# The low halves of a weight stream: an adding DMA from GpSimd's queue instead of a subtraction on VectorE

## The chip, the cores and the metric

One core of one Trainium2 chip runs the whole kernel. The metric is the device time of one execution in microseconds, lower is better; it was run three times before the change. The engines are named as the profile names them: PE is TensorE (its weight loads are PEld), DVE is VectorE, ACT is ScalarE, POOL is GpSimd, SP is SyncE, whose queue issues the DMAs of the kernel before.

## What is computed

Two layers of a diffusion transformer over 256 context tokens and 256 latent tokens with 1024 features. A layer is a feed-forward half step, a hybrid mixer (a gated linear recurrence, latent attention and neighbourhood attention) and a second feed-forward half step. In the last layer the context is not needed behind the mixer, so the second feed-forward there runs on the 256 latents alone. Cut to what matters here:

```python
for layer in range(2):
    last = layer == 1
    h  = h  + 0.5 * g1  * swiglu(modulate(rms_norm(h),  sh1,  sc1),  ffn1_w_in, ffn1_w_out)
    hc = hc + 0.5 * cg1 * swiglu(modulate(rms_norm(hc), csh1, csc1), ffn1_w_in, ffn1_w_out)
    yc, yl = hybrid_mixer(..., need_ctx=not last)
    h  = h  + gm * yl
    h  = h  + 0.5 * g2 * swiglu(modulate(rms_norm(h), sh2, sc2), ffn2_w_in, ffn2_w_out)
    if not last:
        hc = hc + cgm * yc
        hc = hc + 0.5 * cg2 * swiglu(modulate(rms_norm(hc), csh2, csc2), ffn2_w_in, ffn2_w_out)
return h
```

The weights are float32. Every product runs on TensorE in the type float32r, which keeps fewer bits. So each weight block is split into a high part, the weight rounded to float32r, and a low part, the weight less its high part, and each activation likewise. A product is three matmuls: high by high, high by low and low by high.

## The kernel before

All weights lie in memory as one stream of 128x128 blocks, in the order of use. `chunks` cuts it into 316 chunks of up to 8 blocks, a [128, 1024] float32 tile of 512 KB each; the chunks are numbered 0 to 315. The last feed-forward holds chunks 250 to 315, the output projection of the second layer's mixer chunks 241 to 249, the input projections of that mixer 223 to 241.

A chunk goes through `Stream` in three steps. `load` (line 327) issues one DMA on SP's queue into one of three `wraw` tiles. `split_hi` (line 334) casts it on ScalarE into a `whi` tile. `split_lo` (line 340) subtracts the high part from the raw tile on VectorE into a `wlo` tile (GpSimd may take it for the first six chunks). `whi` and `wlo` come from a ring of five pairs. The raw tile is free for the next load behind the subtraction; a ring pair is free when TensorE has read the chunk's last block. `mm3` (lines 628 to 630) makes the three matmuls of a block: `wh` by `h`, `wh` by `lo`, `wl` by `h`.

A block's three matmuls move 512 columns where both kinds of tokens are worked on, and 256 or 258 in the layer-1 output projection and in the last feed-forward, which have the latents alone. Each block there is taken from the ring once.

Beside the stream, the modulation vectors are made by `gemv`: a [128, 1024] tile `graw` of `w_mod` comes by a DMA on SP's queue, and VectorE multiplies it with silu(c) twice with a sum (`junk`, line 680). There are 144 such tiles, spread over the first three feed-forwards and the start. GpSimd takes the few powers of the norms (`rr`, `rq`, line 743) and some sums of squares (`acc`, line 723).

The order of each engine's instructions is fixed when the program is built. `Weave` runs a small model of the engines over programs of steps, each with an engine, a cost, the events it waits for and fires and the slots it takes and gives (`raw` 3, `ring` 5), and emits the step that could start first or is most urgent. On the chip each engine then works through its queue in that order, with semaphores for the waits.

Of the kernel before, what the change touches and what calls it, by code (L numbers as in the profile page):

```python
# [24 lines left out]
AF = mybir.ActivationFunctionType  # L25
# [21 lines left out]
# ---------------------------------------------------------------- layout of the weight stream  # L47

def out_tiles(l, w):
    """Tiles of a feed-forward output, by what is worked on together: the latents alone leave little time per tile."""  # L50
    return ((0, 1),) + tuple((dt,) for dt in range(2, KT)) if (l, w) == (L - 1, 2) else tuple((dt,) for dt in range(KT))


def plan():
    """The order of 128-wide weight blocks in the stream: (key, blocks side by side)."""
# [36 lines left out]
def uses(key):  # L92
    """How often the blocks of a key are taken from the ring."""
# [17 lines left out]
def chunks(pl):  # L111
    """Cut the stream into chunks of up to CH blocks; no group straddles two chunks."""
# [159 lines left out]
def pack_gates(a):  # L272
    """Two 64-wide blocks on the diagonal of each 128 x 128 tile: [layer, tile, 128, dir, a or x, 128]."""
# [28 lines left out]
# ---------------------------------------------------------------- the kernel  # L302

class Stream:
    """Weights in order of use: DMA, then the exact split into two float32r parts."""
# [30 lines left out]

    def split_lo(self, i, eng):
# [14 lines left out]
class Step:  # L352
    """One step of a program: its engine and cost (or several that could do it), what it emits, the events it waits
    for and fires (when its data lands, lag later), the slots it takes first and gives back."""
# [7 lines left out]
class Weave:  # L362
    """Interleaves programs (generators of steps) in the order in which a model of the engines runs them.

    A step may run once its events have fired and its slots are free; of those that could start first on an
    engine, the one of the most urgent program is emitted. Each engine then issues in the order of emission.
    """

    LATENCY = {"PE": 0.2, "ACT": 0.135, "DVE": 0.135, "POOL": 0.19, "DMA": 0.0}
# [22 lines left out]
    def pace(self, t):  # L392
        """The tensor engine's clock halves after a window of little work, until a window of full work."""
# [6 lines left out]
    def start(self, p):  # L400
        """(start, program, engine, cost) of the next step, or None."""
# [85 lines left out]
def emit(tc, xT, cc, wmod, wst, cols_d, cst_d, nab, gates, wm0, ccol, out, layers=L):  # L487
# [3 lines left out]
    with es:  # L491
# [30 lines left out]
        def S(*a, **k):  # L522
            return Step(*a, **k)
# [1252 lines left out]
```

## Time and profile before

| | |
|---|---|
| three runs | 1764.41, 1761.28, 1764.37 us, median 1764.37 |
| span of the profiled execution, first to last instruction | 1759.8 us (its time as a run is not listed apart; the median stands 4.6 us above the span) |
| PE busy | 1735.3 us, 99% |
| DVE busy | 1194.3 us, 68% |
| ACT busy | 696.3 us, 40% |
| POOL busy | 82.8 us, 5% |
| DMA, mean share of 16 engines | 41% on queue q1, 143 GB/s |

The busy shares are means over stages that differ. Two kinds of answers are read below: the busy times of every engine within a stretch of the span, and the DMA queue of such a stretch, whose share is that of 16 DMA engines and whose rate in GB/s stands beside it. A matmul's busy time overlaps with that of its neighbours, so PE's pace is read from the number of matmuls in a stretch.

### The profile page before, as it was taken

To read this page: it belongs to the slowest core of one execution; us is meant where nothing else is said; L and a number is where in the kernel's file an instruction comes from. 1 tells how busy PE (TensorE), PEld (TensorE's weight loads), DVE (VectorE), ACT (ScalarE), POOL (GpSimd) and SP (SyncE) were. 2 spreads that over 40 slices of the span, in tenths; PEclk is the share of its full clock that TensorE was granted. 3 is DMA by queue.
4 is the path that set the end of the run, shared out by engine and by line. 5 is a ranking of instruction groups with operands and counts; after the bars stand their busy time and mean duration, and the time that the engine had idled before them with its cause. 6 is when DMAs were issued, how large, how long until landed. Compare 5 with 4: busy or idle time off the path is not lost.

```text
span 1759.8 us, 24027 instructions
## 1 busy us (share of the span) xinstructions
PE 1735.3 (99%) x9428; PEld 1426.8 (81%) x9428; DVE 1194.3 (68%) x1958; ACT 696.3 (40%) x1096; POOL 82.8 (5%) x68
## 2 busy tenths in 40 slices
PE   7999999999999999999999999999999999999999
PEld 4788888889766698888888898888888977699999
DVE  7898677636667778776775478776333667876564
ACT  4432122224667553221222252222222367764442
POOL 1100000000110010000000000000000111100000
PEclk9999999999999999999999999999999999999999
DMA  8554445322221126554553345444222132246653
GB/s 323 194 202 180 166 180 188 136 95 91 78 69 42 49 85 216 184 186 167 187 183 129 112 160 183 182 174 151 96 96 96 63 112 90 65 129 192 183 183 123
DMA packets 73589, 251.71 MB, mean 143 GB/s; under 512 B 9090, under 2 KB 12418, under 8 KB 73220
## 3 DMA queue, kind: packets, MB, share of 16 engines
q1 hardware_dynamic: 73476, 250.18, 41.0%
q8 instruction: 74, 1.21, 0.3%
q14 instruction: 39, 0.32, 0.1%
HBM read 249.10 MB, written 1.05 MB: 142 GB/s over the span
## 4 chain that ended last, share of the span: by engine, by line
PE 94%; DVE 3%; ACT 1%; issue 1%; POOL 0%; DMA 0%; SPq 0%; DVEq 0%; POOLq 0%; ACTq 0%
PE mm L628 27%; PE mm L629 27%; PE mm L630 27%; PE sc L1256 3%; PE tr L1282 1%; PE o L1326 1%; PE mm L1388 1%; DVE junk L1678 1%; PE tr L949 1%; PE o L628 1%; PE o L629 1%; PE o L630 1%; PE sc L1008 1%; PE mm L1507 1%; PE sc L628 1%
## 5 line engine op out<-in xcount | busy, mean ns | idle before, releaser
L628 PE MATMUL mm<-xh,whi 128*128 128x512 f32 (+2 forms) x1722 | 627.8, 365 | 2.6 <-ACT xh L770 2.5
L629 PE MATMUL mm<-xl,whi 128*128 128x512 f32 (+2 forms) x1722 | 613.2, 356 | 2.9 <-DVE xl L1461 1.6
L630 PE MATMUL mm<-xh,wlo 128*128 128x512 f32 (+2 forms) x1722 | 612.8, 356 | 0.0
L334 ACT CAST whi<-wraw 128x1024 fp32r<-128x1024 f32 (+1 forms) x316 | 330.4, 1046 | 666.9 <-PE mm L629 458.2
L340 DVE TENSOR_TENSOR wlo<-wraw,whi 128x1024 fp32r<-128x1024 f32 (+1 forms) x311 | 379.8, 1222 | 260.3 <-ACT whi L334 256.7
L628 PEld LDWEIGHTS mm<-xh,whi 128*128 128x128 f32 x1722 | 325.8, 189 | 65.7 <-issue 12.5
L629 PEld LDWEIGHTS mm<-xl,whi 128*128 128x128 f32 x1722 | 326.0, 189 | 55.8 <-issue 4.1
L630 PEld LDWEIGHTS mm<-xh,wlo 128*128 128x128 f32 x1722 | 325.7, 189 | 50.7
L680 DVE SCALAR_TENSOR_TENSOR junk<-graw,silc 128x1024 f32<-128x1024 f32 x256 | 312.7, 1221 | 4.9 <-DMA graw<-in_wmod_dram 0.5
L628 PE MATMUL mm<-hh,whi 128*128 128x512 f32 (+1 forms) x748 | 264.6, 354 | 0.0
L629 PE MATMUL mm<-hl,whi 128*128 128x512 f32 (+1 forms) x748 | 263.1, 352 | 0.0
L630 PE MATMUL mm<-hh,wlo 128*128 128x512 f32 (+1 forms) x748 | 262.2, 351 | 0.0
L630 PEld LDWEIGHTS mm<-hh,wlo 128*128 128x128 f32 x748 | 140.6, 188 | 21.8
L628 PEld LDWEIGHTS mm<-hh,whi 128*128 128x128 f32 x748 | 140.3, 188 | 21.3
L629 PEld LDWEIGHTS mm<-hl,whi 128*128 128x128 f32 x748 | 140.8, 188 | 20.5
L804 DVE SCALAR_TENSOR_TENSOR x<-mm,mod,x 128x256 f32<-128x256 f32 x158 | 71.2, 479 | 89.1 <-PE mm L630 88.6
L846 ACT CAST hh<-h 128x512 fp32r<-128x512 f32 (+1 forms) x88 | 49.7, 567 | 156.2 <-DVE h L834 133.8
L834 DVE TENSOR_TENSOR h<-sg,mm 128x512 f32<-128x512 f32 x62 | 42.6, 686 | 69.9 <-PE mm L630 69.3
L857 DVE TENSOR_TENSOR hl<-h,hh 128x512 fp32r<-128x512 f32 (+1 forms) x88 | 54.5, 623 | 33.0 <-ACT hh L846 32.8
L723 POOL TENSOR_TENSOR acc<-acc,nsq 128x256 f32<-128x256 f32 x18 | 19.1, 1064 | 1090.1 <-ACT nsq L719 1090.0
L1256 PE MATMUL sc<-m_kp,m_qp 128*128 128x512 f32 (+3 forms) x120 | 55.8, 546 | 1.5 <-ACT m_p L1273 1.0
L743 POOL TENSOR_TENSOR rr<-rv,nhalf 128x2 f32<-128x2 f32 (+2 forms) x29 | 37.6, 1304 | 320.0 <-DVE rv L736 243.1
(234 smaller groups left out, 1484.7 us busy)
## 6 DMA issues: line engine op xcount, KB each, us to landing
wraw<-in_wst_dram SPq DMA_DIRECT2D x308, 512.0 KB, 3.4
graw<-in_wmod_dram SPq DMA_DIRECT2D x137, 512.0 KB, 5.3
graw<-in_wm_dram SPq DMA_DIRECT2D x7, 512.0 KB, 7.2
x<-in_xT_dram SPq DMA_DIRECT2D x8, 256.0 KB, 5.3
nab<-in_nab_dram SPq DMA_DIRECT2D x16, 128.0 KB, 2.1
silc<-in_cc_dram SPq DMA_DIRECT2D x2, 1024.0 KB, 5.5
m_gw<-in_gates_dram SPq DMA_DIRECT2D x6, 256.0 KB, 2.7
out_dram<-x SPq DMA_DIRECT2D x8, 128.0 KB, 1.9
```

The source lines that it names most:

```text
L334: self.nc.scalar.copy(hi[:, :n], self.raws[i][:, :n])
L340: eng.tensor_tensor(lo[:, :n], self.raws.pop(i)[:, :n], hi[:, :n].bitcast(F32), OP.subtract)
L628: PE.matmul(o, wh[:, :m], h, start=start, stop=False)
L629: PE.matmul(o, wh[:, :m], lo, start=False, stop=False)
L630: PE.matmul(o, wl[:, :m], h, start=False, stop=stop)
L680: V.scalar_tensor_tensor(ph["junk"], g["r"], 1.0, ph["sc"][:, s, :], OP.mult, OP.mult, accum_out=mod[l, c][:, s, j:j + 1])
L743: G.tensor_tensor(r, v, e, OP.pow)
L804: yield S("DVE", 0.4, lambda: V.scalar_tensor_tensor(x[:, dt, half(s)], o[:, half(s)], gate[:, s, dt:dt + 1], x[:, dt, half(s)], OP.mult, ...
L834: V.tensor_tensor(g["h"][:, cs], g["s"][:, cs], pu[:, cs], OP.mult)
L846: A.copy(hs[f][0][:, cs], g["h"][:, hc])
L857: yield S("DVE", dve(n), lambda: V.tensor_tensor(hs[f][1][:, cs], g["h"][:, hc], hs[f][0][:, cs].bitcast(F32), OP.subtract), give={"h": 1} ...
L1256: PE.matmul(g["s"][:, :keys], q[r0:r1, ts(t)], kk[r0:r1, :keys], start=True, stop=True)
```

## The change

From chunk 12 on, the low part is made in two steps. ScalarE writes the negated rounded weight into `wlo`, straight from the raw tile, behind its cast into `whi`; then a DMA issued on GpSimd's queue adds the raw weights, read from memory a second time, to what lies in `wlo`. The raw tile is given back behind the negation. Chunks 0 to 11 keep the subtraction. In the planner the new DMA is a step of an engine of its own, SW, with a cost of 1.5 and a landing 3.0 later.

```diff
 class Stream:
+    def negate(self, i):
+        n = self.size(i)
+        hi, lo = self.tiles[i]
+        self.nc.scalar.activation(lo[:, :n], self.raws.pop(i)[:, :n], AF.Copy, scale=-1.0)
+
+    def add_raw(self, i):
+        n = self.size(i)
+        hi, lo = self.tiles[i]
+        src = bass.AP(tensor=self.src.tensor, offset=self.src.offset + self.off[i], ap=[[n, 128], [1, n]])
+        self.nc.gpsimd.dma_start(lo[:, :n], src, accum_op=OP.add)
...
-    LATENCY = {"PE": 0.2, "ACT": 0.135, "DVE": 0.135, "POOL": 0.19, "DMA": 0.0}
+    LATENCY = {"PE": 0.2, "ACT": 0.135, "DVE": 0.135, "POOL": 0.19, "DMA": 0.0, "SW": 0.0}
...
-SLACK = {"PE": 0.12, "ACT": 0.12, "DVE": 0.12, "POOL": 0.0, "DMA": 0.0}
+SLACK = {"PE": 0.12, "ACT": 0.12, "DVE": 0.12, "POOL": 0.0, "DMA": 0.0, "SW": 0.0}
...
+N_VECTOR = 12
...
         def split_hi(cs):
             for c in cs:
                 yield S("ACT", act(W.size(c)), lambda: W.split_hi(c), take={"ring": 1},
                         wait=[("raw", c)] + ([("hi", c - 1)] if c else []), fire=("hi", c))
+                if c >= N_VECTOR:
+                    yield S("ACT", act(W.size(c)), lambda: W.negate(c), give={"raw": 1}, fire=("nhi", c))

         def split_lo(cs):
             for c in cs:
                 n = W.size(c)
+                if c >= N_VECTOR:
+                    yield S("SW", 1.5, lambda: W.add_raw(c), wait=[("nhi", c)], fire=("chunk", c), lag=3.0)
+                    continue
                 yield S(("DVE", "POOL") if c < N_POOL else ("DVE",), (dve(n), 2.3), lambda e=None: W.split_lo(
                     c, G if e == "POOL" else V), wait=[("hi", c)], give={"raw": 1}, fire=("chunk", c))
```

Comments were taken out of the file as well, and the new lines shift the line numbers behind them. In the changed kernel the cast stays on line 334, the negation is line 341, the adding DMA line 348, the subtraction line 353.

ScalarE's queue in the last feed-forward, before (the silu of the gate is `sg`, the high part of the product `hh`):

```order
L334 CAST whi<-wraw 128x1024
L846 CAST hh<-h 128x256
L334 CAST whi<-wraw 128x1024 x2
L853 ACTIVATE sg<-sg 128x256
L334 CAST whi<-wraw 128x1024
L846 CAST hh<-h 128x256
```

and with the change:

```order
L334 CAST whi<-wraw 128x1024
L341 ACTIVATE wlo<-wraw 128x1024
L334 CAST whi<-wraw 128x1024
L872 ACTIVATE sg<-sg 128x256
L341 ACTIVATE wlo<-wraw 128x1024
L865 CAST hh<-h 128x256
```

Each cast of a chunk is followed by a negation of the same size, with at most a `sg` or a `hh` between them.

GpSimd's queue from the end of the layer-1 mixer to the end of the program, before:

```order
L743 TENSOR_TENSOR rr<-rv,nhalf 128x8
L743 TENSOR_TENSOR rq<-rv,nhalf 128x2
L723 TENSOR_TENSOR acc_12846<-acc_12846,nsq 128x256 x2
L743 TENSOR_TENSOR rr<-rv,nhalf 128x2
L1771 UNCONDITIONAL_BRANCH
```

and with the change:

```order
L762 TENSOR_TENSOR rr<-rv,nhalf 128x8
L348 DMA wlo<-in_wst_dram 128x1024 x2
L762 TENSOR_TENSOR rq<-rv,nhalf 128x2
L348 DMA wlo<-in_wst_dram 128x1024 x7
L762 TENSOR_TENSOR rr<-rv,nhalf 128x2
L348 DMA wlo<-in_wst_dram 128x1024 x61
L348 DMA wlo<-in_wst_dram 128x768
L1790 UNCONDITIONAL_BRANCH
```

The adding DMAs, 304 in all, now stand in GpSimd's queue between the powers; behind the last norm's power there are 62 in a row.

## Rows read from the trace of the kernel before

**Rows 1.** The page, parts 1 and 2: busy time by engine; 40 slices.

```profile
PE 1735.3 (99%) x9428; PEld 1426.8 (81%) x9428; DVE 1194.3 (68%) x1958; ACT 696.3 (40%) x1096; POOL 82.8 (5%) x68
...
PE   7999999999999999999999999999999999999999
...
DMA  8554445322221126554553345444222132246653
GB/s 323 194 202 180 166 180 188 136 95 91 78 69 42 49 85 216 184 186 167 187 183 129 112 160 183 182 174 151 96 96 96 63 112 90 65 129 192 183 183 123
```

**Rows 2.** Stretches: us, busy us by engine (instructions), PE clock, DMA share, GB/s.

```profile
88.00:308.00 220.00, 220.00 (x942) 176.91 (x941) 172.97 (x260) 56.90 (x68) 0.00 (x0) 1.00 0.51 183
396.00:660.00 264.00, 263.46 (x1627) 203.34 (x1626) 184.96 (x374) 162.86 (x303) 29.36 (x25) 1.00 0.20 69
660.00:924.00 264.00, 264.00 (x1169) 214.12 (x1168) 200.24 (x294) 71.80 (x91) 0.00 (x0) 1.00 0.52 187
1056.00:1232.00 176.00, 176.00 (x754) 141.51 (x753) 129.73 (x191) 42.97 (x52) 0.00 (x0) 1.00 0.47 172
1232.00:1364.00 132.00, 132.00 (x565) 106.14 (x564) 46.02 (x54) 36.87 (x50) 1.46 (x1) 1.00 0.28 96
1364.00:1580.00 216.00, 209.91 (x1449) 170.75 (x1448) 158.77 (x316) 136.08 (x252) 26.94 (x23) 1.00 0.29 89
1540.00:1584.00 44.00, 43.50 (x349) 40.72 (x348) 34.77 (x69) 26.88 (x49) 2.47 (x3) 1.00 0.40 127
1584.00:1750.00 166.00, 166.00 (x1386) 166.00 (x1385) 104.51 (x150) 73.12 (x96) 0.00 (x0) 1.00 0.58 178
```

**Rows 3.** Waits of PE between 1364 and 1580 us: total, times, longest.

```profile
PE mm L629 <- DVE xl L1461: 1.6, 1, 1.6
PE sc L1256 <- ACT m_p L1273: 1.0, 1, 1.0
```

**Rows 4.** The page, part 5: groups of instructions, busy, mean ns, idle before.

```profile
L334 ACT CAST whi<-wraw 128x1024 fp32r<-128x1024 f32 (+1 forms) x316 | 330.4, 1046 | 666.9 <-PE mm L629 458.2
L340 DVE TENSOR_TENSOR wlo<-wraw,whi 128x1024 fp32r<-128x1024 f32 (+1 forms) x311 | 379.8, 1222 | 260.3 <-ACT whi L334 256.7
```

**Rows 5.** ACT in order of time, 1640 to 1648 us: start, duration, instruction.

```profile
1641.83 1.05 ACT L334 CAST whi<-wraw 128x1024 fp32r<-128x1024 f32 x1 [1.83 <-PE mm L629]
1644.71 1.05 ACT L334 CAST whi<-wraw 128x1024 fp32r<-128x1024 f32 x1 [1.83 <-PE mm L629]
```

**Rows 6.** Waits of ACT between 1584 and 1756 us: total, times, longest.

```profile
ACT whi L334 <- PE mm L629: 46.7, 27, 1.8
...
ACT whi L334 <- DMA wraw<-in_wst_dram: 2.4, 2, 1.3
```

**Rows 7.** DMA queues and issues between 12 and 27 us; last figure us to landing.

```profile
DMA packets 1721, 6.20 MB, mean 413 GB/s; under 512 B 190, under 2 KB 210, under 8 KB 1721
...
q1 hardware_dynamic: 1721, 6.20, 102.7%
...
wraw<-in_wst_dram SPq DMA_DIRECT2D x3, 512.0 KB, 7.7
```

**Rows 8.** The same between 1232 and 1364 us.

```profile
q1 hardware_dynamic: 3456, 12.58, 27.4%
...
wraw<-in_wst_dram SPq DMA_DIRECT2D x23, 512.0 KB, 3.2
```

**Rows 9.** The same between 1584 and 1750 us.

```profile
DMA packets 8710, 29.62 MB, mean 178 GB/s; under 512 B 960, under 2 KB 1657, under 8 KB 8697
...
q1 hardware_dynamic: 8697, 29.42, 57.8%
...
wraw<-in_wst_dram SPq DMA_DIRECT2D x53, 512.0 KB, 3.5
```

**Rows 10.** POOL's instructions by shape over the span: busy, mean ns, idle before.

```profile
L340 POOL TENSOR_TENSOR wlo<-wraw,whi 128x1024 fp32r<-128x1024 f32 x5 | 13.4, 2684 | 23.6 <-ACT whi L334 23.6
...
L743 POOL TENSOR_TENSOR rr<-rv,nhalf 128x4 f32<-128x4 f32 x5 | 6.7, 1341 | 73.8 <-DVE rv L736 73.8
```

## Prediction

> **What bounds the kernel now.** I read the page first [rows 1]: PE is busy 99% of the span and in every slice but the first, while DVE, from which the change takes work, stands at 68%. So the first question is not how much DVE time goes, but whether PE ever waits for DVE or for a chunk. The waits of PE answer it: they are short. In the second mixer, the one stretch with gaps, PE is idle for 216.0 - 209.9 = 6.1 us [rows 2], and only two of its waits reach 1 us [rows 3]. None of them is for a `wlo`. That is all that a relieved DVE can give back outside the start and the end.
>
> The second question is the pace at which PE eats chunks, stage by stage, because the change makes the supply dearer. A chunk of 8 blocks is 24 matmuls. With 512 columns the three stretches with modulation tiles hold 942 + 1169 + 754 = 2865 matmuls in 660 us [rows 2], so a chunk lasts 5.53 us. In the last feed-forward it is 1386 matmuls in 166 us [rows 2], so **a chunk lasts 2.87 us**; the casts start 2.88 us apart there [rows 5]. The layer-1 output projection runs at about that pace (349 matmuls in 44 us, 3.0 us a chunk [rows 2]).
>
> The third is what the DMA engines do. Over the span they stand at 41%, but by stretch it is 0.51 in the first feed-forward, 0.28 where no modulation tile is loaded, and 0.58 in the last feed-forward [rows 2]. The ceiling shows at the start, where the queue is never empty: 413 GB/s at a share of 102.7% [rows 7]. One 512 KB chunk (524,288 bytes) at that rate costs 1.27 us of all 16 engines. Where the queue has gaps, packets take longer: 27.4% of 132 us over 23 chunks is 1.57 us a chunk [rows 8], and 57.8% of 166 us over 29.42 MB is 1.71 us for 512 KB [rows 9].
>
> **The change, part by part.**
>
> *Removed:* 304 subtractions on DVE, 1.22 us each [rows 4], 371 us of DVE time. PE waits for none of them, so this is worth 0 on the path, with an end at -6.1 us if every gap of the second mixer closes.
>
> *Added on ACT:* 304 negations. The nearest row is the cast of the same tile, 1.05 us [rows 4], 319 us in all. In the last feed-forward ACT goes from 73.1 of 166 us to about 73 + 58 x 1.05 = 134 (166 / 2.87 = 58 chunks): 81%, not full. In the second mixer it goes from 136.1 of 216 to 163, with 26 chunks: 76%. There ACT's results are waited for as much as DVE's [rows 3], so bounds are -6 and, if each negation lay on the path, +27; I take 0, as DVE loses 26 x 1.22 = 32 us in the same stretch. The order of ACT's queue shows a negation behind each cast; what stands behind it, `sg` or `hh`, comes up to 1.05 us later, and tiles of two gates are in flight to cover that.
>
> *Added latency of a chunk.* A cast waits for its ring pair, not for data: 46.7 us of waits on PE against 2.4 us on the load [rows 6]. From there PE has four other chunks to eat, 4 x 2.87 = 11.5 us. In that time now must pass: cast 1.05, negation 1.05, the issue on POOL (no row shows one; POOL's power on a 128x4 tile takes 1.34 [rows 10], taken as an estimate) and the landing, between 3.5 us [rows 9] and 7.7 us under a full queue [rows 7]. That makes 6.9 to 11.1 us. It fits, with little left at the upper end; with 512 columns there are 22 us. POOL's queue is in order, and behind the last norm 62 adds stand in a row with no power among them, so no late DVE result holds them up there. In the mixers powers and adds hold each other up by an issue or two, at 3 us or more a chunk: 0.
>
> *Added on the DMA engines.* This is the term that counts. Each of 304 chunks is read from memory again, and the old content of `wlo` has to be read too before the sum is written. No row shows such a DMA. From below it costs what a load costs, 1.27 us; from above two loads at the slowest packets, 2 x 1.71 = 3.42 us. I take **two loads at the full rate, 2.54 us**, since two tiles are read for one written and the engines will be full where it matters, which is the state of rows 7.
>
> What I can read is a stream of loads at 413 GB/s [rows 7]. The Trainium skill (Collectives: The Full Stack, The bandwidth ceiling) lays the half rate of a reduce on its two source reads, and not on the addition. By that rule the price is the 2.54 us that I took and the time 1830; by the row alone, one stream, it would be 1764. No run here shows it yet.
>
> In the last feed-forward and the output projection ahead of it, one chunk then needs 1.27 + 2.54 = 3.81 us of all DMA engines, and PE eats it in 2.87: DMA becomes the bound, by 0.94 us a chunk. The stretch holds chunks 241 to 315, 75 of them; five wait in the ring when it begins, so 70 x 0.94 = **+65 us**. With 512 columns and modulation tiles the share is (0.51 + 0.52 + 0.47) / 3 = 0.50 of 5.53 us, 2.77 us; with 2.54 more it is 5.31 of 5.53, just hidden: 0. Without modulation tiles there is more room.
>
> *Sum.* The profile's span is 1759.8 us and the median run stands 4.6 us above it, which I carry over: 1759.8 + 65 + 4.6 = 1829.4, said as **1830 us**, 3.7% above the median of 1764.4.
>
> Bounds of the sum: with the add at 1.27 us a chunk needs 2.54 of 2.87 us, nothing is added, and the mixer's gaps end the lower side at 1758. With load and add at the slow packets, 1.71 + 3.42 = 5.13 us, the last stage gains 70 x 2.26 = 158 us, and the stages with modulation tiles need 2.77 + 3.42 = 6.19 of 5.53 us over 2865 / 24 = 119 chunks, +79 us: 2001 us.
>
> **The rivals.**
>
> *Hidden transfer (not slower).* The add decides: under 2.87 - 1.27 = 1.60 us a chunk it fits beside the load in the last feed-forward and nothing moves: 1764 us, or down to 1758 if the mixer's 6 us also go. For it: 42% of the DMA time is free there [rows 9], and the reading of `wlo` may overlap with that of the weights. Against it: even then the engines are 88% full, and the landing nears the 7.7 us of a full queue. A second way to the same time: all data of this kernel comes by one queue, q1 [rows 7 to 9], so the rows cannot say whether GpSimd's queue finds room of its own. If it did, 1.27 and 2.54 would run side by side below 2.87, and the time were 1764 us. The Trainium skill (DMA: Bandwidth & Descriptors, Issuing engines are not separate DMA queues) says that DMAs of all issuers run on the same 16 engines and interleave; by that the sum is 1830 and not 1764, and no run here shows it yet. Chance of no change 0.11, of faster 0.04.
>
> *Latency alone.* The rate suffices, but a chunk lands later than 11.5 us behind its cast's release. Five ring pairs then pace PE: at 14 us of latency the period is (14 + 2.87) / 5 = 3.37 us, 70 x 0.50 = 35 us, 1799 us; less for a smaller miss. For it: 11.1 us at the upper end above. Against it: the median landing is 3.5 us at a share of 0.58 [rows 9]. Chance 0.09, for 1768 to 1799.
>
> *Dear add.* Above 5.53 - 2.77 = 2.76 us the stages with modulation tiles fall behind too, and the time runs to the upper bound, 2001 us. For it: outside a full queue packets do take 1.57 to 1.71 us for 512 KB [rows 8, 9], and reading back what is to be written may keep fewer packets in flight. Against it: the modulation tiles can come later without PE waiting for them at once. Chance 0.20.
>
> *POOL's issue becomes the bound.* It decides above 2.87 us an add. POOL's dearest row, a subtraction of such a tile, takes 2.68 [rows 10], and its small powers 1.34, so at either the queue keeps up; at twice the dearest, 5.4 us, it would be 70 x 2.5 = +175 us, 1940 us. Chance 0.05.
>
> That the change doesn't do what it says is not one: 304 adding DMAs stand in POOL's queue, and 12 subtractions are left.
>
> **How the numbers follow.** The forecast, with the add between 2.1 and 2.76 us (1799 to 1845 us), has 0.51, the dear add 0.20, latency alone 0.09, POOL 0.05, no change 0.11, faster 0.04. About 0.2%, 3.5 us, is what a measurement of this kernel can tell from no change. So slower by more has 0.85. The range goes from 1766, which leaves out the faster case and most of no change (0.13), to 2010, just above the upper bound of the costs, which leaves 0.05 for prices beyond the rows.
>
> **What would show it.** Right: in the last feed-forward the DMA share goes from 0.58 to 0.95 or more, with a second queue beside q1; PE waits for the add of its chunk (`wlo`) there and nearly nowhere else; casts start about 3.8 us apart; DVE falls to some 820 us, ACT rises to some 1015; the first three feed-forwards keep their length. Packets of the new queue take about twice as long as those of q1. Wrong: a last feed-forward that keeps its 2.87 us a chunk; waits for adds with 512 columns; a POOL that is busy nearly all of the last stage while DMA has gaps; or PE waits in the mixers that end at ACT.

## The result and the profile after

The changed kernel takes **1887.86 us** in the median (1879.41 to 1893.18), against 1764.03 us (1761.28 to 1764.41) for the kernel before in the same series. The ratio is 1.070, with a 95% interval from 1.0685 to 1.0716. The profiled execution spans 1888.4 us, 128.6 us more than the 1759.8 of before. The direction and the place of the largest loss were as predicted; the size was not, by 58 us.

The page, parts 1 and 2, answers to [rows 1]:

```profile
PE 1781.4 (94%) x9428; PEld 1446.1 (77%) x9428; DVE 857.5 (45%) x1688; ACT 970.4 (51%) x1373; POOL 334.2 (18%) x365
...
PE   7999999999998999999999999999999898988887
...
DMA  8699999975444369999999699998886555899998
```

DVE gave up 337 us and ACT took on 274, where 371 and 319 were costed: ACT has 27 instructions fewer than its 1096 and the 304 negations, DVE 34 more than its 1958 less 304, so the planner has given some other work to DVE. PE, which showed nines from the second slice on, now has eights in the mixers (slice 13 and slices 32 and 34) and in the last feed-forward. The digits of DMA show four plateaus, one for each feed-forward; during the first three this view shows no loss of PE. To size each place I cut both traces at the cast of the same chunk, so that a stage holds the same work in both (us):

| stage (its casts) | before | after | more |
|---|---|---|---|
| first feed-forward (0 to 70) | 404.7 | 405.1 | +0.4 |
| first mixer (71 to 96) | 235.5 | 264.3 | +28.8 |
| second feed-forward (97 to 162) | 372.7 | 380.6 | +7.9 |
| third feed-forward (163 to 228) | 372.7 | 382.8 | +10.1 |
| second mixer (229 to 245) | 117.6 | 134.8 | +17.2 |
| output projection (246 to 254) | 49.6 | 50.5 | +0.9 |
| last feed-forward (255 to 314) | 168.4 | 235.7 | +67.3 |
| ahead of the first cast and behind the last | 38.6 | 34.6 | -4.0 |

(A cast runs five ring pairs ahead of PE: the cast of chunk 71 falls where PE begins on chunk 66, the mixer's first. The sum is +128.6.) So 67 us came in the last feed-forward, 46 in the mixers and 18 in the two later feed-forwards with modulation tiles.

The two mixers in the windows view, before; columns as in [rows 2]:

```profile
426.00:662.00 236.00, 235.46 (x1390) 175.34 (x1389) 166.35 (x331) 151.45 (x280) 26.22 (x21) 1.00 0.20 68
...
1407.00:1525.00 118.00, 114.04 (x721) 83.60 (x721) 90.79 (x180) 88.40 (x163) 17.56 (x13) 1.00 0.29 90
```

and the five later stages of the changed kernel, without the output projection:

```profile
427.00:691.00 264.00, 246.29 (x1384) 179.99 (x1383) 142.44 (x313) 173.56 (x302) 48.60 (x47) 0.95 0.47 110
691.00:1071.00 380.00, 373.61 (x1755) 306.70 (x1755) 180.27 (x324) 168.34 (x212) 60.13 (x71) 1.00 0.94 252
1071.00:1454.00 383.00, 377.92 (x1762) 310.62 (x1761) 140.88 (x256) 166.51 (x208) 60.23 (x71) 0.99 0.90 225
1454.00:1589.00 135.00, 122.55 (x731) 88.29 (x732) 76.01 (x176) 94.03 (x156) 32.38 (x32) 0.95 0.59 143
1640.00:1875.00 235.00, 192.72 (x1469) 181.06 (x1468) 41.62 (x102) 136.93 (x165) 51.79 (x60) 0.99 1.05 272
```

Three kinds of stage can be read off the last columns. In the last feed-forward the DMA share is 1.05, all there is, and DVE and ACT have room: that stage is bound by DMA. In the mixers the share is only 0.47 and 0.59, yet PE is idle for 264.00 - 246.29 = 17.7 us in the first, where it had 0.5 before, and its granted clock is 0.95. On the mean the mixers are therefore not short of bandwidth, but the mean hides bursts: in 40 slices of 1 us, from 420 to 460 us, the DMA engines stand near full for some 16 us and nearly at rest around them.

```profile
DMA  9821000004978989899999999961000005995783
```

Between the two lie the feed-forwards with modulation tiles, at 0.94 and 0.90, with 6.4 and 5.1 us of idle PE.

**The last feed-forward, in two views.** ScalarE's timeline, where a bracket is the idle time ahead and what ended it:

```profile
1703.22 1.05 ACT L334 CAST whi<-wraw 128x1024 fp32r<-128x1024 f32 x1 [1.36 <-DMA wraw<-in_wst_dram]
...
1707.04 1.05 ACT L334 CAST whi<-wraw 128x1024 fp32r<-128x1024 f32 x1 [1.81 <-DMA wraw<-in_wst_dram]
...
1710.83 1.04 ACT L334 CAST whi<-wraw 128x1024 fp32r<-128x1024 f32 x1 [1.09 <-DMA wraw<-in_wst_dram]
```

The casts stand 3.8 us apart where they stood 2.88 apart [rows 5], and these three wait for their data, where they waited for a ring pair [rows 6]; over the stage ScalarE's casts wait 58.9 us for data and 37.2 us for PE. The DMA queues between 1660 and 1860 us, against [rows 9]:

```profile
DMA packets 15015, 54.73 MB, mean 274 GB/s; under 512 B 1670, under 2 KB 1695, under 8 KB 15001
...
q0 software_dynamic: 7482, 27.25, 69.1%
q1 hardware_dynamic: 7519, 27.28, 35.7%
...
wraw<-in_wst_dram SPq DMA_DIRECT2D x52, 512.0 KB, 9.3
wlo<-in_wst_dram POOLq DMA_DIRECT2D x52, 512.0 KB, 9.7
```

The adds are queue q0. It moves the same bytes as the loads in q1 and takes 69.1% against 35.7%. Per chunk of 524,288 bytes that is 0.691 x 200 us x 0.524 / 27.25 = **2.66 us** for an add and 1.37 us for a load, together 4.03 at a total share of 105%. At 100% it would be 3.84, near the spacing of the casts above; over the stage the mean is 235.7 / 60 = 3.93 us. Behind cast 266 the steady pace is 3.83, against 2.88 in the kernel before. In the stage's first eleven chunks it is 4.0 against 2.5: before, the casts catch up there after a gap of 7.5 us, which they can't do now. What that adds to the stage comes back in the main behind the last cast (-4.0 in the table). GpSimd is busy for 51.79 of 235 us there, so its issue does not set the pace.

**Where PE waits.** The longest waits of PE over the whole span: total, times, longest.

```profile
PE mm L649 <- DMA wlo<-in_wst_dram: 44.7, 59, 4.5
PE mm L1407 <- DMA m_gw<-in_gates_dram: 7.5, 2, 4.4
PE mm L647 <- ACT hh L865: 5.8, 2, 3.2
PE tr L1301 <- ACT m_p L1292: 5.7, 2, 3.0
PE mm L647 <- DVE sg L857: 4.6, 1, 4.6
PE mm L647 <- DVE xh L1009: 4.3, 2, 4.1
```

The first row is in the main the last feed-forward (36.9 us in 54 waits there, the longest 1.3). The others are few, and most are long. That matters, as the next view shows: PE's clock behind such a wait, in three windows of 6 us,

```profile
1188.00:1194.00 6.00, 3.31 (x15) 2.32 (x13) 5.53 (x9) 0.13 (x1) 0.00 (x0) 0.97 1.06 277
1194.00:1200.00 6.00, 5.46 (x12) 4.09 (x13) 2.34 (x4) 4.29 (x5) 1.72 (x2) 0.50 0.99 307
1200.00:1206.00 6.00, 6.00 (x26) 4.79 (x26) 4.58 (x9) 2.01 (x2) 0.58 (x1) 0.96 1.03 273
```

and PE's own timeline there:

```profile
1190.92 0.39 PE L649 MATMUL mm<-hh,wlo 128*128 128x512 f32 x1
1194.54 0.80 PE L647 MATMUL mm<-hh,whi 128*128 128x512 f32 x1 [3.24 <-ACT hh L865]
1195.27 0.80 PE L648 MATMUL mm<-hl,whi 128*128 128x512 f32 x1
1195.86 0.63 PE L649 MATMUL mm<-hh,wlo 128*128 128x512 f32 x1
...
1200.53 0.40 PE L648 MATMUL mm<-hl,whi 128*128 128x512 f32 x1
```

PE stood still for 3.24 us and then worked for 6 us at a granted clock of 0.50, the 1.2 GHz level. Between 1194.54 and 1200.53 13 matmuls passed, which take 13 x 0.233 = 3.0 us at the spacing of those ahead of the wait. So this wait of 3.2 us cost some 3.0 us more behind it. The short waits of the last feed-forward did not: between 1716 and 1848 us the granted clock is 1.00.

**Who makes `hh` late.** In this wait ScalarE had itself waited, for DVE's product `h`:

```profile
1186.01 0.58 ACT L849 ACTIVATE sg<-mm 128x512 f32<-128x512 f32 x1
...
1193.87 0.62 ACT L865 CAST hh<-h 128x512 fp32r<-128x512 f32 x1 [7.29 <-DVE h L853]
```

DVE's queue holds the products `h` between the `junk` of the modulation tiles, and those wait for their data. DVE's own timeline, with three more `junk` left out between the two:

```profile
1188.20 1.23 DVE L699 SCALAR_TENSOR_TENSOR junk<-graw,silc 128x1024 f32<-128x1024 f32 x1 [5.18 <-DMA graw<-in_wmod_dram]
...
1193.16 0.68 DVE L853 TENSOR_TENSOR h<-sg,mm 128x512 f32<-128x512 f32 x1
```

ScalarE's `sg` was done at 1186.6, and its product came 6.6 us later. The page, groups of instructions, and behind them the DMA issues with the median us from issue to landing:

```profile
L699 DVE SCALAR_TENSOR_TENSOR junk<-graw,silc 128x1024 f32<-128x1024 f32 x256 | 313.5, 1224 | 286.9 <-DMA graw<-in_wmod_dram 281.1
...
wlo<-in_wst_dram POOLq DMA_DIRECT2D x296, 512.0 KB, 8.9
graw<-in_wmod_dram SPq DMA_DIRECT2D x137, 512.0 KB, 10.1
```

A modulation tile lands after 10.1 us, against 5.3 before. DVE had been relieved of 337 us of work and now spends 281 us waiting for `graw`, with finished gate halves standing behind the wait. In the second feed-forward ScalarE's waits for `h` grew from 66.3 to 104.2 us, the longest from 3.7 to 14.6.

### The profile page after: what moved, and what is told of

It reads as the page before. It is cut to its first block, busy times and chain, and to the rows that moved or that the text cites. A ratio compares the mean times of both kernels' runs of the same rounds, so it can differ in the third digit from the quotient of the medians.

```text
span 1888.4 us, 24704 instructions
## 1 busy us (share of the span) xinstructions
PE 1781.4 (94%) x9428; PEld 1446.1 (77%) x9428; DVE 857.5 (45%) x1688; ACT 970.4 (51%) x1373; POOL 334.2 (18%) x365
## 3 DMA queue, kind: packets, MB, share of 16 engines
q1 hardware_dynamic: 73476, 250.18, 38.6%
HBM read 407.96 MB, written 1.05 MB: 217 GB/s over the span
## 4 chain that ended last, share of the span: by engine, by line
PE 64%; DMA 19%; issue 6%; DVE 5%; ACT 5%; POOL 0%; SPq 0%; ACTq 0%; POOLq 0%; DVEq 0%
PE mm L647 19%; PE mm L649 18%; PE mm L648 18%; DMA graw<-in_wmod_dram 6%; DMA wlo<-in_wst_dram 6%; DMA wraw<-in_wst_dram 5%; ACT wlo L341 2%; PE sc L1275 2%; DVE junk L699 2%; DMA m_gw<-in_gates_dram 1%; PE tr L1301 1%; ACT whi L334 1%; PE mm L1407 1%; DVE junk L1697 1%; PE o L1345 1%
## 5 line engine op out<-in xcount | busy, mean ns | idle before, releaser
L649 PE MATMUL mm<-xh,wlo 128*128 128x512 f32 (+2 forms) x1722 | 620.9, 361 | 25.3 <-DMA wlo<-in_wst_dram 25.3
L348 POOL DMA_DIRECT2D wlo<-in_wst_dram x304 | 264.2, 869 | 1330.3 <-ACT wlo L341 1206.2
L647 PEld LDWEIGHTS mm<-xh,whi 128*128 128x128 f32 x1722 | 329.8, 192 | 81.3 <-issue 13.3
L648 PEld LDWEIGHTS mm<-xl,whi 128*128 128x128 f32 x1722 | 330.1, 192 | 53.7 <-issue 3.8
L341 ACT ACTIVATE wlo<-wraw 128x1024 fp32r<-128x1024 f32 (+2 forms) x304 | 319.3, 1050 | 0.0
L649 PEld LDWEIGHTS mm<-hh,wlo 128*128 128x128 f32 x748 | 141.2, 189 | 39.5 <-DMA wlo<-in_wst_dram 17.8
L647 PEld LDWEIGHTS mm<-hh,whi 128*128 128x128 f32 x748 | 141.2, 189 | 28.1 <-ACT hh L865 6.6
L860 DVE SCALAR_TENSOR_TENSOR h<-h,sg 128x256 f32<-128x256 f32 x22 | 10.6, 484 | 109.3 <-ACT sg L872 109.3
## 6 DMA issues: line engine op xcount, KB each, us to landing
graw<-in_wmod_dram SPq DMA_DIRECT2D x137, 512.0 KB, 10.1
x<-in_xT_dram SPq DMA_DIRECT2D x8, 256.0 KB, 4.8
m_gw<-in_gates_dram SPq DMA_DIRECT2D x6, 256.0 KB, 4.9
```

What stands on the lines that cost most here:

```text
L341: self.nc.scalar.activation(lo[:, :n], self.raws.pop(i)[:, :n], AF.Copy, scale=-1.0)
L348: self.nc.gpsimd.dma_start(lo[:, :n], src, accum_op=OP.add)
L647: PE.matmul(o, wh[:, :m], h, start=start, stop=False)
L648: PE.matmul(o, wh[:, :m], lo, start=False, stop=False)
L649: PE.matmul(o, wl[:, :m], h, start=False, stop=stop)
```

## The experiments

Two theories of the loss in the mixers and the feed-forwards stood open: that the adding DMA is dear and late, and that the negations in ScalarE's in-order queue hold back what PE needs. Each experiment is given with its stage lengths, cut as above (us):

| kernel | first mixer | second ff | third ff | second mixer | out-proj. | last ff | span |
|---|---|---|---|---|---|---|---|
| before | 235.5 | 372.7 | 372.7 | 117.6 | 49.6 | 168.4 | 1759.8 |
| after | 264.3 | 380.6 | 382.8 | 134.8 | 50.5 | 235.7 | 1888.4 |
| plain copy | 245.1 | 372.7 | 372.7 | 120.5 | 48.1 | 179.2 | 1782.0 |
| no second DMA, sum on VectorE | 251.9 | 372.6 | 372.5 | 125.6 | 59.1 | 176.8 | 1802.3 |
| negation on VectorE | 256.6 | 392.8 | 385.6 | 138.5 | 48.8 | 236.4 | 1901.0 |
| planner told of the add | 256.0 | 382.7 | 383.9 | 147.2 | 50.9 | 235.7 | 1896.8 |
| adds not in the last stage | 260.9 | 383.9 | 380.0 | 128.1 | 57.6 | 174.4 | 1828.6 |
| adds not in the mixers | 236.4 | 384.9 | 385.2 | 119.1 | 47.0 | 236.2 | 1849.0 |
| adds in the mixers only | 266.4 | 372.6 | 373.2 | 135.5 | 58.4 | 174.4 | 1824.2 |
| adds in the last stage only | 235.5 | 372.6 | 372.7 | 119.1 | 48.4 | 236.1 | 1823.9 |
| 3 of 4 adds of the last stage | 235.5 | 372.7 | 372.7 | 118.6 | 48.6 | 208.4 | 1798.3 |
| half the adds of the last stage | 235.5 | 372.7 | 372.7 | 119.7 | 48.4 | 180.3 | 1771.8 |
| adds in quiet stretches only | 235.5 | 372.7 | 372.7 | 117.2 | 51.4 | 168.4 | 1761.0 |

**What the addition itself costs: a plain copy in its place.** Everything else of the change stays: the negation, the queue, the bytes, the tile that is written, the order of the instructions. The kernel leaves out the addition, so its low parts hold the raw weights. (POOL issues such a copy in 0.54 us, an add in 0.87.)

```diff
-        self.nc.gpsimd.dma_start(lo[:, :n], src, accum_op=OP.add)
+        self.nc.gpsimd.dma_start(lo[:, :n], src)
```

> The DMA on GpSimd's queue copies the raw weights over the low part where the change adds them; the negation stays, so every engine has the same instructions and the low parts hold raw weights. Theory A (the add is dear because it reads the low tile back): the second queue's price falls from 2.66-2.75 us per 512 KB to 1.3-1.6 us, the last feed-forward goes from 236 us (casts of chunks 255 to 315) back to 168-180, the stages with modulation tiles lose their 8 and 10 us, total 1765-1815 depending on what the mixers keep. Theory B (any second copy of the stream on a second queue costs this, whatever it does): the price stays above 2.4 us and the total above 1865 us.

Measured: 1785.88 us, ratio 1.0133 [1.0103, 1.0162]. The DMA queues of this kernel between 88 and 308 us,

```profile
q1 hardware_dynamic: 10963, 39.92, 51.0%
q0 software_dynamic: 5616, 20.45, 25.8%
```

and of the changed kernel in the same stretch:

```profile
q1 hardware_dynamic: 10811, 39.38, 52.0%
q0 software_dynamic: 5590, 20.40, 48.6%
```

A copied chunk takes 0.258 x 220 x 0.524 / 20.45 = 1.455 us of all engines, an added one 0.486 x 220 x 0.524 / 20.40 = 2.75 us, 1.9 times as much. The loads of q1 cost the same in both. So the price lies in adding, neither in GpSimd's queue nor in a second reading of the weights. With the copy the two feed-forwards return to 372.7 us, which shows that their +18 us come from the adding alone; in the second, ScalarE's waits for `h` fall from 104.2 to 56.7 us, below the 66.3 of before. The mixers keep 9.6 + 2.9 = 12.5 of their 46 us. Of the three long waits of PE in the first mixer, for a `wlo`, for the gate weights `m_gw` and for an `xh` (the high part of an activation), the copy removes the first two and leaves the third (427 to 672 us):

```profile
PE mm L647 <- DVE xh L1009: 4.1, 1, 4.1
```

The last feed-forward keeps 10.8 us, but not by its pace: behind cast 266 the casts stand 2.88 us apart, as before, and that part takes 141.2 us, against 141.1. 10.6 us come in the first eleven chunks, where PE waits once in the whole stage and the clock falls behind it (two windows of 15 us):

```profile
PE mm L647 <- DVE sg L857: 5.9, 1, 5.9
...
1590.00:1605.00 15.00, 10.18 (x83) 9.76 (x81) 1.60 (x5) 10.02 (x11) 2.31 (x5) 0.97 1.04 363
1605.00:1620.00 15.00, 13.89 (x98) 13.89 (x99) 5.79 (x15) 10.69 (x16) 1.59 (x3) 0.81 0.69 238
```

VectorE made this `sg` late because it had waited 13.1 us for ScalarE, whose queue has its step of the gate behind five casts and their negations, and four of these casts waited for their raw tiles. The changed kernel has such a wait too (4.6 us, among the longest above), but there it costs nothing more: with the negations on VectorE, two experiments on, it is gone, and the stage takes 236.4 us all the same.

**ScalarE's share: the negation kept, the second DMA taken away.** VectorE adds the raw tile to the negated high part, so the raw tile is given back there.

```diff
-                    yield S("SW", 1.5, lambda: W.add_raw(c), wait=[("nhi", c)], fire=("chunk", c), lag=3.0)
+                    yield S("DVE", dve(n), lambda: W.add_dve(c), wait=[("nhi", c)], give={"raw": 1}, fire=("chunk", c))
...
+        self.nc.vector.tensor_tensor(lo[:, :n], lo[:, :n].bitcast(F32), self.raws.pop(i)[:, :n], OP.add)
```

> ScalarE negates as in the change, but VectorE adds the raw tile to the negated part, with no DMA; the raw tile is given back behind that addition. Theory A (the mixers' 46 us come from DMAs that land late behind the adds and from GpSimd's queue): mixers within 8 us of before, total 1764-1775 us. Theory C (ScalarE, now 319 us fuller and with a negation ahead of each evacuation, costs the mixers their 46 us): mixers keep 25-46 us, total 1790-1810 us. Last feed-forward 168-172 us by both.

Measured: 1803.18 us, ratio 1.0231 [1.0201, 1.0261]. The mixers keep 16.4 + 8.0 = 24.4 us without any second DMA, just under the range expected for ScalarE's part. PE's waits there are others than in the changed kernel (the longest are 3.1 us for VectorE and 2.8 us for ScalarE). The last two stages have 9.5 and 8.4 us more, where at most 4 us was expected for the last feed-forward. There PE waits twice, early in each of them:

```profile
PE mm L652 <- DVE xh L1014: 5.1, 1, 5.1
PE mm L652 <- DVE sg L862: 4.9, 1, 4.9
```

These two waits may be the work of VectorE's queue and of the order built for this variant, which was not separated. The +24.4 of the mixers has VectorE loaded as before the change, a raw tile held longer and an order of its own in it, so it does not measure ScalarE's part alone; the 12.5 of the plain copy, whose second DMA is cheap but not free, is another reading of it.

**The negation on VectorE instead.** The adding DMA stays, and ScalarE's queue is as it was before.

```diff
-        self.nc.scalar.activation(lo[:, :n], self.raws.pop(i)[:, :n], AF.Copy, scale=-1.0)
+        self.nc.vector.tensor_scalar(lo[:, :n], self.raws.pop(i)[:, :n], -1.0, None, OP.mult)
...
-                    yield S("ACT", act(W.size(c)), lambda: W.negate(c), give={"raw": 1}, fire=("nhi", c))
...
+                    yield S("DVE", dve2(n), lambda: W.negate(c), wait=[("hi", c)], give={"raw": 1}, fire=("nhi", c))
```

> The adding DMA stays for every chunk from 12 on, but VectorE writes the negated high part (a one-operand multiply by -1 from the raw tile) instead of ScalarE. Theory C (about 16 of the first mixer's 29 us come from the negations in ScalarE's queue, as in the run without DMAs): casts of chunks 71 to 97 take 244-252 us instead of 264, 229 to 246 about 125-128 instead of 135, total 1855-1875 us. Theory D (the late landing of the adds alone is at fault): 260 us or more there, total 1880-1895 us. Last feed-forward near 236 us by both.

Measured: 1903.39 us, ratio 1.0797 [1.0766, 1.0829], worse than the change and above both expectations. The first mixer got 8 us back, the second none (+20.9), and the second feed-forward rose to 392.8: now the negations themselves stand in VectorE's queue, where `junk` waits 111.1 us for modulation tiles between 700 and 1000 us. With ScalarE's queue free of negations the mixers still lose 42 us, though some of that may be new, from VectorE's queue. In the first mixer the wait for an `xh` is gone, and those for `m_gw` (3.3 us) and a `wlo` (3.0 us) stay: the counterpart of the plain copy. The theory that ScalarE's queue is the larger part finds no support here.

**A better order: the planner told of the add.** It had counted the add as 1.5 us of an engine of its own with a landing 3.0 later. Here it counts 0.9 us of POOL and a landing 9.0 later, about what the trace shows.

```diff
-                    yield S("SW", 1.5, lambda: W.add_raw(c), wait=[("nhi", c)], fire=("chunk", c), lag=3.0)
+                    yield S("POOL", 0.9, lambda: W.add_raw(c), wait=[("nhi", c)], fire=("chunk", c), lag=9.0)
```

> The same instructions as the change, but the planner counts an add as 0.9 us of GpSimd and lets it land 9.0 us later (the trace's 0.87 and 8.9) instead of 1.5 us of an engine of its own and 3.0. Theory E (the mixers and the stages with modulation tiles lose their time because the planned order rests on adds that land 6 us too early): the mixers (71 to 97 and 229 to 246) come within 20 us of before in sum instead of 46, total 1845-1865 us. Theory F (the loss is one of capacity, of ScalarE's and the DMA engines' time, that no order mends): mixers within 10 us of the change's, total 1878-1895 us.

Measured: 1890.25 us, ratio 1.0723 [1.0609, 1.0837], the same as the change within the interval. The first mixer gains 8 us and the second loses 12. A truer model did not cure the mixers.

**The adds by stage.** The next kernels make the low part the new way in some chunks only, and by subtraction in the others:

```diff
-                if c >= N_VECTOR:
+                if adds(c):
```

with `adds(c)` in both places. *Not in the output projection and the last feed-forward* (`N_VECTOR <= c < 241`):

> The adding DMA serves chunks 12 to 240 alone; the output projection of the second layer and the last feed-forward (chunks 241 to 315) are split by subtraction as before. Theory A (a saturated DMA in the last stage is the first term): casts of chunks 255 to 315 take 168-172 us instead of 236, total 1888 - 67 = 1821 us (1815-1828). If the loss there were only handed on from a late second mixer: the stage would keep more than 190 us and the total more than 1840.

Measured: 1832.34 us, ratio 1.0396 [1.0366, 1.0426]. The last feed-forward falls to 174.4 us, 61 of its 67 us gone; the mixers and the other two feed-forwards keep 35.9 and 18.5. The miss against the expected total is in the output projection, +8.0, where PE waits once for 5.1 us, for an `xh` of VectorE, and in +6.0 behind it.

*Not in the mixers* (without chunks 66 to 91 and 223 to 240, those that PE reads there; the first range has the output projection of its layer in it, from chunk 83 on):

> The adding DMA serves every chunk from 12 on but those of the mixers' input projections (66 to 91 and 223 to 240), which are subtracted as before. If the mixers' own adds and negations cost their 46 us: the stretch from the cast of chunk 71 to that of chunk 97 goes from 264 us back to 236-240, that from 229 to 246 from 135 to 118-122, total about 1842 us (1838-1850). If the cost comes in from the neighbouring stages (gate weights and bias tiles late behind others' adds): at least 20 of the 46 us stay, total 1860-1888.

Measured: 1845.99 us, ratio 1.0474 [1.0408, 1.0539]. The mixers are back within 0.9 and 1.5 us. So what they lose comes from the chunks that are made in them, not from the feed-forwards around them.

*In the mixers only:*

> The adding DMA serves the mixers' input projections alone (chunks 66 to 91 and 223 to 240), the counterpart of the run that leaves them out. If the mixers' loss is made by their own adds and negations: casts of chunks 71 to 97 take 255-268 us and 229 to 246 128-140, total 1764 + 46 = 1810 us (1795-1815). If adds of the neighbouring stages are needed for it (full engines at the way in and out): less than half of it, total below 1787 us.

Measured: 1822.12 us, ratio 1.0330 [1.0309, 1.0352]. The mixers lose 30.9 and 17.9 us, the whole of it, with 44 adds and the rest of the stream untouched. The total misses its expectation by 7 us, for the last two stages lose 8.8 and 6.0 us as well, though none of their chunks has an add; the first of these kernels has much the same there (8.0 and 6.0). PE's waits between 400 and 720 us name three causes at equal length:

```profile
PE mm L1413 <- DMA m_gw<-in_gates_dram: 4.2, 1, 4.2
PE mm L653 <- DVE xh L1015: 4.1, 1, 4.1
PE mm L655 <- DMA wlo<-in_wst_dram: 4.1, 1, 4.1
```

The same three stand at nearly the same lengths in the changed kernel's first mixer. Two steps of the critical chain there, with a stretch left out between them, show what made the load and the add late: start, duration, what.

```profile
431.75 11.75 DMA m_gw<-in_gates_dram
...
478.67 10.88 DMA wlo<-in_wst_dram
```

A 256 KB load of gate weights, issued beside four adds, landed after 11.75 us, where its fellow of before took 3.8; and an add landed after 10.88 us. Both fall into bursts in which the DMA engines are near full (the digits above show the first, to 446 us; the second lasts from 478 to 491). Two us ahead of that add, POOL had sat idle for 12.46 us until a negation came; the casts and negations of both chunks stood late in ScalarE's queue, behind copies that wait for PE. The `xh` is another matter: the chain to it goes through VectorE, which works without a gap from 595.40 until the cast into `xh` ends at 604.33, and the same wait stands in the plain copy's kernel, while it is absent where VectorE negates. It goes with ScalarE's fuller queue and the order planned around it, not with the DMA engines; which of the two was not tried.

*In the output projection and the last feed-forward only* (`c >= 241`), *3 of 4 there* (`c % 4`), and *half of them* (`c % 2`):

> The adding DMA serves chunks 241 to 315 alone (second layer's output projection and last feed-forward); all others are subtracted as before. Theory A (DMA time of the last stage, 3.93 us a chunk): casts of chunks 255 to 315 take 234-238 us, both mixers within 3 us of before, total 1764 + 67 = 1831 us (1825-1840). If the last stage's loss came from what is handed on by the mixers, it would fall below 200 us, total below 1800.

> Of chunks 241 to 315 three in four get the adding DMA, all other chunks of the kernel are subtracted. By the account of DMA time a chunk needs 1.37 + 0.75 x 2.66 = 3.37 us, 0.50 more than the 2.87 that TensorE takes: casts of chunks 255 to 315 take 202-210 us (half gave 180, all 236), total 1793-1803 us. If the loss did not go with the engines' time but set in at once where adds land late: 225 us or more, total above 1815 us.

> Of chunks 241 to 315 only the odd ones get the adding DMA; all other chunks of the kernel are subtracted as before. By the account of DMA time (1.37 us a load and 2.66 an add at full engines) a chunk needs 1.37 + 2.66 / 2 = 2.70 us on the mean, less than the 2.87 that TensorE takes: casts of chunks 255 to 315 take 168-176 us, total 1762-1774 us. If the late landing of each add (9 us) paced TensorE through the five ring pairs rather than the engines' time: 185-205 us, total 1780-1800 us.

Measured: 1826.44 us, ratio 1.0361 [1.0331, 1.0391]; 1796.45 us, ratio 1.0185 [1.0165, 1.0205]; 1770.49 us, ratio 1.0048 [1.0024, 1.0072]. The last feed-forward takes 236.1, 208.4 and 180.3 us, so 3.94, 3.47 and 3.01 us a chunk. The last two quarters of the adds cost 0.46 to 0.47 us a chunk each, less than a quarter of 2.66 us, since the prices fall as the mix gets richer in adds: with three in four, a load takes 1.43 and an add 2.73 us at a total share of 102% (1610 to 1770 us). With half the adds, between 1600 and 1750 us,

```profile
q1 hardware_dynamic: 7332, 26.29, 50.1%
q0 software_dynamic: 3562, 12.95, 47.1%
```

a load takes 1.50 us and an add 2.86, and 1.50 + 2.86 / 2 = 2.93 us stands just above PE's pace of 2.88. The stage's 180.3 us lie between the two expectations: the account with fixed prices (2.70 us a chunk, 176 us at most) was 4 us too low, and a pace set by the landing, 185 us or more, did not come. With the prices measured in each run the account by DMA time holds along the line: the engines stand at 97 to 105%, and the cost grows with the number of adds.

*In quiet stretches only*: 46 chunks of the feed-forwards that meet no modulation tiles, with 512 columns.

> The adding DMA serves 46 chunks alone (54 to 63, 142 to 155, 200 to 221), all in feed-forward stretches with 512 columns whose modulation tiles are done, where the DMA engines stand at 0.28 to 0.36; the rest is subtracted. By the account of DMA time a chunk needs 1.4 + 2.7 = 4.1 of 5.5 us there. Theory A (the subtractions taken off VectorE, 46 x 1.22 = 56 us, were hidden, and the adds are hidden too): the same as before within 0.2%, 1761-1768 us. If VectorE's relief were worth something by itself: below 1760 us. If the late landing alone costs: above 1770 us.

Measured: 1762.94 us against 1763.82, ratio 0.9997 [0.9988, 1.0006]. Where the DMA engines have room and PE takes 5.5 us a chunk, the add is hidden. But taking 56 us from VectorE (46 x 1.22) gives nothing back either. An add takes 7.7 us to land there in the median, and PE does not wait for it.

## Why the prediction was right, and where it fell short

**DMA as the bound of the last feed-forward: right.** Predicted were a share of 0.95 or more, a second queue with packets about twice as long, casts some 3.8 us apart, and +65 us. Measured: 1.05, 69.1% against 35.7% for equal bytes, 3.83 us in the steady part, and +67.3 + 0.9 us in the two stages. By their share of the engines both parts were taken a little low: the add at 2.54, where it takes 2.66 to 2.75 us, and the load at 1.27, where it takes 1.37 (by share, [rows 7] give 1.30: 1.027 x 15 us x 0.524 / 6.20). But as the total share stands at 105%, load and add together last 3.84 us, against the 3.81 of the prediction. The excess of a chunk was right, 0.95 us where 0.94 was forecast. The count of chunks was right by luck: the output projection takes 5.5 us a chunk in the kernel before (49.6 / 9, by its casts) and not the 3.0 that were read off its matmuls, so it lost only 0.9 us, and 75 chunks less five came close to the 66 of the last feed-forward alone. The choice of two streams for the price was right, and the plain copy shows that it is the sum, not the queue. That agrees with the Trainium skill (Collectives: The Full Stack, The bandwidth ceiling), which lays the half rate of a reduce on its two source reads: 1.9 here. That it is the reading of `wlo`, and not the addition itself, which takes the time is the page's account of a reduce, carried over to this DMA; no run here separates the two.

**One set of engines for both queues: right.** The rival in which GpSimd's queue finds room of its own fell: both shares sum to 105%, and the loads land after 9.3 us where they took 3.5 [rows 9]. The Trainium skill says so too (DMA: Bandwidth & Descriptors, Issuing engines are not separate DMA queues), and the trace agrees.

**VectorE's relief worth nothing: right,** shown for the quiet stretches alone. In the mixers, where the forecast saw up to 6.1 us, other losses cover it, and no run separates it.

**Latency alone: not the bound.** A chunk's way is now 1.05 + 1.05 + 0.87 + 9.7 = 12.7 us, longer than the 11.1 us of the forecast's upper end and than the 11.5 us that the ring covers. By the forecast's own formula that gives (12.7 + 2.88) / 5 = 3.1 us a chunk, as an estimate, and 3.83 were measured.

**POOL's issue: not the bound.** An add takes POOL 0.87 us:

```profile
L348 POOL DMA_DIRECT2D wlo<-in_wst_dram x304 | 264.2, 869 | 1330.3 <-ACT wlo L341 1206.2
```

**"5.31 of 5.53, just hidden: 0": failed,** by 18 us in the second and third feed-forward. The measured need, 2.77 + 2.75 = 5.52 us, left no room in 5.53 and little in the 5.65 us that a chunk takes by the casts (372.7 / 66), as the account feared only for an add above 2.76 us; the dear-add rival had the mechanism half. The step that failed is reading a mean share as if transfers came evenly, and asking only who waits for the adds. PE waited there for a `wlo` once, for 1.3 us. What came late was another load, the modulation tile; it held up VectorE's in-order queue, and behind it `h`, `hh` and PE, and then the clock. The plain copy, with the same queue and bytes, removes all of it. The first feed-forward, just as full (52.0% + 48.6%), lost only 0.4 us; ScalarE waits 1.6 us for `h` there, not 104.2. Why its order is so much more patient was not tried.

**"In the mixers powers and adds hold each other up by an issue or two: 0": failed,** by 46 us, the larger miss. The bounds there were made of VectorE's gaps and ScalarE's negations; the adds' transfers had no part in them, since the share was low (0.20, 0.29 before). But the adds come in bursts that fill the engines for 13 to 16 us, and a small load or an add that PE needs next lands within them. Shown: the loss comes with the mixers' own adds and negations (without them +2.4, with them alone +48.8); the larger part goes with the adding (46.0 to 12.5 us when the copy replaces the add; 42 us remain when the negations leave ScalarE). In the first mixer the waits for `m_gw` and `wlo` go with it, and the wait for `xh` with the negations in ScalarE's queue and the order made for them. The exact split of the microseconds stays open. Two of the forecast's own signs of being wrong were seen here: a wait for an add with 512 columns (4.5 us in the first mixer), and waits that end at ACT (for `m_p`, 2.7 us in the first mixer and 3.0 in the second).

**The clock: not in the sum at all.** The mean granted clock over the span went from 0.998 to 0.982. As an estimate, (1 - 0.982) x 1888.4 = 34 us against 0.002 x 1759.8 = 4 us: some 30 of the 129 us may be matmuls at the lower level. In the first mixer 17.7 - 0.5 = 17.2 us are idle PE; of the other 11.6, the clock's 0.05 x 264 = 13 us is about the whole. The one wait followed above, of 3.24 us, cost nearly twice its length; waits of up to 1.3 us in the last feed-forward did not slow the clock.

**The sum redone.** 1829.4 + 46.0 for the mixers + 18.0 for the feed-forwards + 3.2 for the last two stages - 3.6 for the first feed-forward, the start and the tail - 5.1, since the new span stands 0.5 above the median and not 4.6 below, makes 1887.9. The parts are not additive across kernels: mixers alone (1824.2 - 1759.8 = 64.4) and last stage alone (64.1) with the 18 of the feed-forwards make 146.5, not 128.6. Of the 18 us between, 14.8 are the +8.8 and +6.0 that the mixers-only kernel has in the last two stages. They may be delays that a stage bound by DMA swallows, or a price of the order in which VectorE subtracts there (the kernel without adds in the last stage, which subtracts there too, has +8.0 and +6.0); no run decides between the two.

No variant beats the kernel before; the best, with adds in quiet stretches, equals it.

## What to carry to other kernels

Price a DMA that adds as nearly two copies, and ask of each stage whether load and add fit into the time that PE takes for a chunk; where they don't, the loss is the difference times the chunks, and can be read off a table. Where they fit on the mean but the engines come near full, for a stage or only for a burst of some 15 us, follow every other load of that stretch: it lands late as well, and what stands behind its consumer in an in-order queue pays. Freeing an engine that nobody waits for returned nothing here, and a wait of PE of some microseconds has to be priced with the slow matmuls behind it.

## What the runs showed of the hardware

An adding DMA from memory into fp32r tiles took 2.66 to 2.86 us of all 16 engines for 512 KB, where a copy from the same queue took 1.455 to 1.48 and a load 1.37 to 1.50. Over the span weight loads beside it landed in 7.7 us instead of 3.4 in the median, and modulation tiles in 10.1 instead of 5.3. In the first mixer, at a mean share of 0.47, a 256 KB load that fell into a burst took 11.75 us, where its fellow of before took 3.8. And behind a wait of 3.24 us PE worked for 6 us at a granted clock of 0.50.
